# A two-layer trunk kernel on one core: float32 products in one matmul each instead of three float32r ones, and a longer ring of weight tiles

## The chip, the core and the metric

The kernel runs on one core of a Trainium2 chip. The core has a matrix engine (TensorE, PE in the profile; its weight loads are shown apart as PEld), a vector engine (VectorE, DVE), a scalar engine (ScalarE, ACT), a general engine (GpSimd, POOL) and SyncE (SP), whose queue issues nearly all of the transfers here. The metric is the device time of one execution in microseconds (us). Before the change it is 2586.55 us, the median of three runs from 2581.08 to 2590.38 us.

## What is computed

256 latent tokens `x` and 256 context tokens `ctx`, each 2048 wide, go through two layers. In both, the tokens are normalized and modulated by a condition vector, multiplied by a wide input matrix, mixed along the sequence, gated, multiplied by an output matrix and added to the stream. Only the latent tokens leave the second layer.

```
# layer 1 of the reference (called layer 0 in the kernel)
hx = modulate(x, norm, sh, sc) @ w_in            # 16 + 24 + 9 column blocks of 128
o_na  = neighbourhood_attention(...)              # 8 heads of 128
o_mla = mla_latent_attention(...)                 # 8 heads, from ranks of 512
x = x + gt * ((concat(o_na, o_mla) * silu(z)) @ w_out)
# layer 2 (layer 1 in the kernel)
h = modulate(x, norm, sh, sc) @ w_in              # keys, queries, values, gates z
q, k, v = silu(depthwise_conv(qkv)), q and k normalized per head
o = gated_delta_chunked(...) in both directions   # 32 heads, chunks of 64 tokens
x = x + gt * ((rmsnorm(o) * silu(z)) @ w_out)
out = rmsnorm(x)
```

Everything is float32. The weights come from memory once, in tiles of 128 rows by 1024 columns.

## The kernel before

Features lie on the 128 partitions and tokens along the free axis, so that one matmul multiplies a 128x128 block of weights by 128x512 activations (both sequences) or 128x256 (latent tokens alone) and adds the product to a PSUM bank. One such block is called a **k-step** below; 16 k-steps make a column block of 128 outputs, 32 in the last output matrix.

The chip's float32 matmul is not used for these products. A weight tile `raw` is rounded by ScalarE to a float32r tile `whi` (line 77) and VectorE makes the remainder `wlo` (line 78); the activations are held as `hh` and `hl` likewise, made in `modulate`. A k-step in `dense` is then three float32r matmuls: high by high (line 90), high by low (line 91), low by high (line 92). `product` (line 346) does the same in the attention, `pd` (line 713) has two such matmuls for the decays, and the state's update in `step` (line 1013) has three for each half of the partitions. Many smaller products are plain float32 already: the permutation `pp` of the rotary embedding (line 434), the sums `pg` (line 660), the modulations `pmod` (line 127), `pks` (line 982), `ptr` (lines 994 and 1027).

The stages in order: the modulations and the gate units `z` of layer 0, in seven groups of feature tiles (`sliced`, up to about 200 us); eight neighbourhood heads, the latent ranks and eight latent heads (`attend`), with the modulation weights of both layers as filler; the output matrix (`gh`, `gl`); modulation 2, which writes `hh` and `hl` anew; the keys and queries of layer 1 (`head`, `inverse`; from about 1130 us on); the scans with the value units as filler (`step`, from about 1800 us on); and the rest of the output matrix.

Outside the scans a scheduler orders each engine's instructions. In the scans (lines 1156 to 1244) PE, VectorE and ScalarE follow the order of the code: `step` yields four times, and between its parts the loop takes 3, 2 and 3 k-steps of a value unit (`cut`). `hi()` and `lo()` make the parts of the next weight tile there, `finish` normalizes and gates a head, stores the result to memory (`god`) and `gate` loads it again and splits it to `gh` and `gl` for the output products. SP's queue runs in order; a load into a tile of a ring waits there until the tile's last reader is done. The ring `raw` has four tiles, `whi` and `wlo` three each.

```
            PE.matmul(ps, wh[:, c], xh[:, k0 + k, sl], start=first and k == 0, stop=False)
            PE.matmul(ps, wh[:, c], xl[:, k0 + k, sl], start=False, stop=False)
            end = PE.matmul(ps, wl[:, c], xh[:, k0 + k, sl], start=False, stop=last and k == kt - 1)
```

Of the kernel before, what the change touches and what calls it, by code (L numbers as in the profile page):

```python
# [16 lines left out]
KT = 16  # L17
S = 256
# [8 lines left out]
def trunk_kernel(ctx: ExitStack, tc: tile.TileContext, g):  # L27
# [4 lines left out]
    wp = ctx.enter_context(tc.tile_pool(name="wp", bufs=2))  # L32
    big = ctx.enter_context(tc.tile_pool(name="big", bufs=1))
# [34 lines left out]
    # ---------------------------------------------------------------- helpers  # L68
    def load_raw(src, n=1024):
        raw = wp.tile([128, 1024], F32, name="raw", tag="raw", bufs=4)  # L70
        nc.sync.dma_start(raw[:, :n], src)
        return raw

    def split(raw, m=1024):
        hi = wp.tile([128, 1024], F32R, name="whi", tag="whi", bufs=3)
        lo = wp.tile([128, 1024], F32R, name="wlo", tag="wlo", bufs=3)
        A.copy(hi[:, :m], raw[:, :m])  # L77
        V.tensor_tensor(lo[:, :m], raw[:, :m], hi[:, :m].bitcast(F32), op=ALU.subtract)  # L78
        return hi, lo

    def load_split(src, n=2048):
        return [split(load_raw(src[:, c:min(n, c + 1024)], min(1024, n - c)), min(1024, n - c))
                for c in range(0, n, 1024)]

    def dense(ps, w, off, kt, xh, xl, k0=0, sl=slice(0, T), first=True, last=True):
        for k in range(kt):
            c = off + k * 128
            wh, wl = w[c // 1024]
            c = slice(c % 1024, c % 1024 + 128)
            PE.matmul(ps, wh[:, c], xh[:, k0 + k, sl], start=first and k == 0, stop=False)  # L90
            PE.matmul(ps, wh[:, c], xl[:, k0 + k, sl], start=False, stop=False)  # L91
            end = PE.matmul(ps, wl[:, c], xh[:, k0 + k, sl], start=False, stop=last and k == kt - 1)  # L92
        return end.ins

    def sliced(wsrc, units, k0, n, xh, xl, pst, first, last):
        # n contraction tiles of two units
        m = 128 * n
        raw = wp.tile([128, 1024], F32, name="raw", tag="raw", bufs=4)
        for e in range(2):
            nc.sync.dma_start(raw[:, m * e:m * e + m], wsrc[units[e]][:, 128 * k0:128 * k0 + m])  # L100
        w = split(raw, 2 * m)
        for e in range(2):
            dense(pst[e], [w], m * e, n, xh, xl, k0=k0, first=first, last=last)
# [1273 lines left out]
```

## Time and profile before

| what | value |
|---|---|
| median of the runs shown | 2586.55 us (2581.08 to 2590.38) |
| span of the profiled execution, first to last instruction | 2580.0 us |
| mean granted TensorE clock in it | 0.985 |
| PE busy from 0 to 70 us | 48.16 us |
| PE busy from 70 to 200 us | 130.00 us |
| PE busy from 1130 to 1800 us (keys and inverses) | 638.54 of 670 us, DVE 594.62, clock 0.96 |
| PE busy from 1800 to 2440 us (scans) | 635.45 of 640 us, DVE 462.61, clock 1.00 |
| PE busy from 2463 to 2570 us (last output products) | 105.10 of 107 us |

The profiled execution has no time of its own beside the span; 6.55 us lie between the span and the median of the timed runs. In the rows of the profile `A*B` is the part of the array that a matmul uses (rows by columns), `128x512 f32` its output, and `xN` a number of records. float32r tiles show as f32 too; the line tells them apart. The end of a matmul's record is modelled, so its duration includes the way through the array, and consecutive records overlap; the time that a matmul holds the engine is read from the distance between starts.

### The profile page before, as it was taken

How to read it: one execution, taken by the hardware profiler on the slowest of the kernel's cores; microseconds unless marked ns; L12 is line 12 of the kernel's file. 1: busy time of each engine (PE TensorE's matmuls, PEld its weight loads, DVE VectorE, ACT ScalarE, POOL GpSimd, SP SyncE). 2: the span in 40 equal slices, each digit the busy share in tenths (PEclk: the TensorE clock that was granted, in tenths of full speed). 3: DMA queues.
4: the chain of work that ended last, by engine and by line, in shares of the span. 5: the costliest groups of instructions: out<-in, count | busy, mean ns of one | idle time of the engine just before them, and what ended most of it. 6: DMA issues, size and time to landing. Idle time of an engine off the chain costs nothing.

```text
span 2580.0 us, 43446 instructions
## 1 busy us (share of the span) xinstructions
PE 2499.2 (97%) x16586; PEld 2039.0 (79%) x16586; DVE 1852.2 (72%) x3543; ACT 1146.6 (44%) x2484; POOL 267.4 (10%) x261
## 2 busy tenths in 40 slices
PE   6999999999999999989999999999999999999998
PEld 4657888888767788768888889897777777777898
DVE  4544788773455687758999999987677777777754
ACT  4223323232333422377656655643444445445353
POOL 0000000000000000133212222310000000003000
PEclk9999999999999999999999999999999999999999
DMA  8872655532343376644454544563333433335454
GB/s 258 289 247 90 201 172 167 175 114 96 117 153 100 120 230 221 212 139 157 142 156 152 160 138 150 159 213 100 88 99 115 119 99 106 113 91 174 153 188 140
DMA packets 201810, 394.30 MB, mean 153 GB/s; under 512 B 68225, under 2 KB 109697, under 8 KB 201473
## 3 DMA queue, kind: packets, MB, share of 16 engines
q1 hardware_dynamic: 200448, 389.98, 47.9%
q8 instruction: 131, 2.15, 0.4%
q10 hardware_dynamic: 1152, 1.54, 0.2%
q14 instruction: 79, 0.64, 0.1%
HBM read 356.28 MB, written 35.13 MB: 152 GB/s over the span
## 4 chain that ended last, share of the span: by engine, by line
PE 79%; DVE 9%; issue 6%; DMA 3%; ACT 2%; SPq 0%; POOL 0%; DVEq 0%; POOLq 0%; ACTq 0%
PE mm L90 19%; PE mm L91 18%; PE mm L92 18%; PE pks L982 3%; PE pmod L127 3%; DVE wlo L78 2%; PE sp L348 2%; PE ptr L994 2%; DVE X L770 1%; DVE outer L768 1%; PE po L348 1%; PE pu L798 1%; DVE acc L561 1%; PE ptr L1027 1%; PE psu L1013 1%
## 5 line engine op out<-in xcount | busy, mean ns | idle before, releaser
L90 PE MATMUL mm<-hh,whi 128*128 128x512 f32 (+1 forms) x2784 | 988.5, 355 | 3.7 <-ACT t L636 2.2
L92 PE MATMUL mm<-hh,wlo 128*128 128x512 f32 (+1 forms) x2784 | 962.2, 346 | 8.7 <-DVE wlo L78 7.5
L91 PE MATMUL mm<-hl,whi 128*128 128x512 f32 (+1 forms) x2784 | 963.2, 346 | 0.0
L77 ACT CAST whi<-raw 128x1024 fp32r<-128x1024 f32 (+2 forms) x346 | 338.3, 979 | 668.4 <-PE mm L91 515.6
L90 PEld LDWEIGHTS mm<-hh,whi 128*128 128x128 f32 x2784 | 535.7, 192 | 113.8 <-issue 32.6
L92 PEld LDWEIGHTS mm<-hh,wlo 128*128 128x128 f32 x2784 | 535.4, 192 | 73.1 <-DVE wlo L78 9.4
L91 PEld LDWEIGHTS mm<-hl,whi 128*128 128x128 f32 x2784 | 536.0, 193 | 62.2 <-issue 8.4
L78 DVE TENSOR_TENSOR wlo<-raw,whi 128x1024 fp32r<-128x1024 f32 (+2 forms) x346 | 402.7, 1166 | 212.9 <-ACT whi L77 206.1
L163 DVE SCALAR_TENSOR_TENSOR lacc<-mraw,cond,lacc 128x512 f32<-128x512 f32 x300 | 208.8, 749 | 0.0
L561 DVE SCALAR_TENSOR_TENSOR acc<-cin,taps,acc 128x508 f32<-128x508 f32 (+3 forms) x256 | 196.1, 767 | 6.7 <-ACT acc L552 4.3
L1004 DVE SCALAR_TENSOR_TENSOR vl<-ptr,egm,vh 128x128 fp32r<-128x128 f32 x224 | 64.6, 346 | 98.3 <-ACT rf L1001 39.4
L711 POOL TENSOR_TENSOR rhs<-ghl,incl 128x512 fp32r<-128x512 f32 (+1 forms) x96 | 108.4, 1139 | 133.4 <-PE pd L713 114.2
L127 PE MATMUL pmod<-mraw,cond 128*32 128x512 f32 (+2 forms) x640 | 94.3, 501 | 23.2 <-DMA mraw<-ab_wm 18.6
L768 DVE SCALAR_TENSOR_TENSOR outer<-L,bv,X 128x31 f32<-128x31 f32 (+15 forms) x248 | 112.4, 453 | 4.7
L1088 DVE TENSOR_TENSOR wlo<-raw,whi 128x1024 fp32r<-128x1024 f32 x84 | 102.6, 1222 | 14.4 <-ACT whi L1080 13.8
L194 POOL TENSOR_TENSOR rs<-ms,half 128x4 f32<-128x4 f32 (+1 forms) x5 | 4.7, 947 | 985.1 <-DVE ms L192 985.1
L770 DVE TENSOR_TENSOR X<-X,outer 128x31 f32<-128x31 f32 (+15 forms) x248 | 101.7, 410 | 4.6
L575 ACT ACTIVATE ac<-acc 128x128 f32<-128x128 f32 x160 | 37.4, 300 | 146.0 <-DVE acc L561 146.0
L90 PE MATMUL mm<-gh,whi 128*128 128x512 f32 x256 | 99.9, 392 | 1.7 <-DVE x1B L493 1.7
L91 PE MATMUL mm<-gl,whi 128*128 128x512 f32 x256 | 99.9, 390 | 0.2 <-DVE gl L481 0.2
L92 PE MATMUL mm<-gh,wlo 128*128 128x512 f32 x256 | 99.7, 390 | 0.0
L998 ACT ACTIVATE vh<-ptr,egm 128x128 fp32r<-128x128 f32 x224 | 71.0, 373 | 56.6 <-PE ptr L994 54.6
(289 smaller groups left out, 3629.2 us busy)
## 6 DMA issues: line engine op xcount, KB each, us to landing
raw<-dn_w SPq DMA_DIRECT2D x194, 512.0 KB, 4.0
mraw<-dn_wm SPq DMA_DIRECT2D x96, 512.0 KB, 4.7
mraw<-ab_wm SPq DMA_DIRECT2D x88, 512.0 KB, 5.4
raw<-ab_w SPq DMA_DIRECT2D x66, 512.0 KB, 3.8
raw<-dn_wo SPq DMA_DIRECT2D x64, 512.0 KB, 3.7
raw<-ab_wo SPq DMA_DIRECT2D x32, 512.0 KB, 4.6
raw<-ab_w SPq DMA_DIRECT2D x32, 256.0 KB, 3.6
spt<-sp SPq DMA_DIRECT2D x64, 128.0 KB, 2.8
```

The lines of the kernel that those rows point to most:

```text
L77: A.copy(hi[:, :m], raw[:, :m])
L78: V.tensor_tensor(lo[:, :m], raw[:, :m], hi[:, :m].bitcast(F32), op=ALU.subtract)
L90: PE.matmul(ps, wh[:, c], xh[:, k0 + k, sl], start=first and k == 0, stop=False)
L91: PE.matmul(ps, wh[:, c], xl[:, k0 + k, sl], start=False, stop=False)
L92: end = PE.matmul(ps, wl[:, c], xh[:, k0 + k, sl], start=False, stop=last and k == kt - 1)
L127: PE.matmul(pmod[32 * q:32 * q + 32, :m], cond[:, 4 * kg + q, :], raw[c // 1024][:, half + c % 1024:half + c % 1024 + m], start=kg == 0, s ...
L163: V.scalar_tensor_tensor(acc[:, s], raw[:, q], cond[:, k, s:s + 1], acc[:, s], op0=ALU.mult, op1=ALU.add)
L561: V.scalar_tensor_tensor(o3[:, :, i0:i1], p3[:, :, i0 + d:i1 + d], taps[:, ch, t:t + 1], o3[:, :, i0:i1], op0=ALU.mult, op1=ALU.add)
L711: P.tensor_tensor(rhs, ghl[i].bitcast(F32)[:, d, kh * 8:kh * 8 + 2 * n].unsqueeze(2).broadcast_to(sh), incl[:, c].unsqueeze(1).broadcast_t ...
L768: V.scalar_tensor_tensor(o, L[:, rows, k:k + 1].broadcast_to([128, n, m]), bv[:, k:k + 1], X[:, k:k + 1, cols].broadcast_to([128, n, m]), ...
L770: V.tensor_tensor(X[:, rows, cols], X[:, rows, cols], o, op=ALU.subtract)
L1088: V.tensor_tensor(w, raws[j], h.bitcast(F32), op=ALU.subtract)
```

## The change

Every product takes its float32 operands as they are. `dense` has one matmul for a k-step; `split`, `hi`, `lo`, `both`, `parts`, `product` and `split_keys` are gone, with all tiles that held low parts. The ring of weight tiles, now the only one, has ten tiles (`RAWS`). `modulate` writes its result with two instructions for each feature tile and sequence, in layer 1 into the tile `x1` that it reads. The output matrix of layer 0 reads the gated outputs `go2` where they are. In layer 1 `finish` writes the gated outputs of all 32 heads into one tile `gob`, which the output products read; the stores to `god`, the loads back and `gate` are gone.

```diff
-    def split(raw, m=1024):
-        hi = wp.tile([128, 1024], F32R, name="whi", tag="whi", bufs=3)
-        lo = wp.tile([128, 1024], F32R, name="wlo", tag="wlo", bufs=3)
-        A.copy(hi[:, :m], raw[:, :m])
-        V.tensor_tensor(lo[:, :m], raw[:, :m], hi[:, :m].bitcast(F32), op=ALU.subtract)
-        return hi, lo
...
-            PE.matmul(ps, wh[:, c], xh[:, k0 + k, sl], start=first and k == 0, stop=False)
-            PE.matmul(ps, wh[:, c], xl[:, k0 + k, sl], start=False, stop=False)
-            end = PE.matmul(ps, wl[:, c], xh[:, k0 + k, sl], start=False, stop=last and k == kt - 1)
+            end = PE.matmul(ps, w[c // 1024][:, c % 1024:c % 1024 + 128], x(k0 + k, sl),
+                            start=first and k == 0, stop=last and k == kt - 1)
...
-        raw = wp.tile([128, 1024], F32, name="raw", tag="raw", bufs=4)
+        raw = wp.tile([128, 1024], F32, name="raw", tag="raw", bufs=RAWS)
...
-                A.activation(hh[:, k, sl], h[:, sl], AF.Identity, bias=shift)
-                if k % 3 == 2:
-                    V.scalar_tensor_tensor(hl[:, k, sl], h[:, sl], shift, hh[:, k, sl].bitcast(F32),
-                                           op0=ALU.add, op1=ALU.subtract)
-                else:
-                    A.activation(h[:, sl], h[:, sl], AF.Identity, bias=shift)
-            if k % 3 != 2:
-                P.tensor_tensor(hl[:, k], h, hh[:, k].bitcast(F32), op=ALU.subtract)
+                V.scalar_tensor_tensor(h[:, k, sl], src(k, s), Am[l][:, k, s:s + 1], rb[:, sl], op0=ALU.mult, op1=ALU.mult)
+                A.activation(h[:, k, sl], h[:, k, sl], AF.Identity, bias=mods[l][:, k, s:s + 1])
...
-                    product(sp[:, :N], lambda i: qT[:, i, q0:q0 + 128], lambda i: kT[:, i, c0:T], True, rope is None)
+                    PE.matmul(sp[:, :N], qT[:, q0:q0 + 128], kT[:, c0:T], start=True, stop=rope is None)
...
-                for i in range(2):
-                    rhs = tp.tile([128, 8, 64], F32R, name="rhs", tag="rhs")[:, :2 * n]
...
-                    PE.matmul(pd, seg[:, c], rhs.rearrange("p u i -> p (u i)"), start=i == 0, stop=i == 1)
+                rhs = tp.tile([128, 8, 64], F32, name="rhs", tag="rhs")[:, :2 * n]
...
+                PE.matmul(pd, seg[:, c], rhs.rearrange("p u i -> p (u i)"), start=True, stop=True)
...
-                for i, (x, y) in enumerate(((0, 0), (0, 1), (1, 0))):
-                    for h in range(2):
-                        r = slice(64 * h, 64 * h + 64)
-                        PE.matmul(psu[h].rearrange("p h v -> p (h v)"), ksp[r, s, x, t],
...
+                for h in range(2):
+                    r = slice(64 * h, 64 * h + 64)
+                    PE.matmul(psu[h].rearrange("p h v -> p (h v)"), o.kt[r, t], vs[r].rearrange("p h v -> p (h v)"),
+                              start=True, stop=True, tile_position=(64 * h, 0))
...
-            o.go = gos[o.kh % 2]
+            o.go = gob[:, 2 * o.kh:2 * o.kh + 2]
...
-            if o.kh < 14:
-                nc.sync.dma_start(god[:, 2 * o.kh:2 * o.kh + 2], o.go)
...
+        def ahead_of(j):
+            while len(raws) < min(len(W), j + RAWS):
+                raws.append(load(W[len(raws)]))
```

The first place is PE's row of work inside the scans, where a value unit's k-steps (`mm`) stand between the parts of a chunk's step: here before the update of the context's state (`pks` and `ptr` from the values `vh`, `vl` and the keys `ksp`). Before:

```order
L90 MATMUL mm<-hh,whi 128x512
L91 MATMUL mm<-hl,whi 128x512
L92 MATMUL mm<-hh,wlo 128x512
L1013 MATMUL pks<-vh,ksp 128x256
L1013 MATMUL ptr<-vh,ksp 128x256
L1013 MATMUL pks<-vl,ksp 128x256
L1013 MATMUL ptr<-vl,ksp 128x256
```

The third pair of the update (high values by low keys) follows, and reads like the first. PE's row at the same kind of place now (`x` is the modulated tile, `kt` the keys as loaded, `ptr<-rh,rc` the end of the latent tokens' chunk):

```order
L1127 MATMUL pvv<-ident,ac_12608 128x128 x4
L81 MATMUL mm<-x_4275,raw 128x512 x2
L953 MATMUL pks<-vh,kt_10529 128x256
L953 MATMUL ptr<-vh,kt_10529 128x256
L81 MATMUL mm<-x_4275,raw 128x512 x3
L966 MATMUL ptr<-rh,rc 128x128 x2
```

A k-step's three rows have become one, and the six of a state's update two; the numbers of k-steps between two parts of the chain (2, then 3) are the same.

The second place is SP's queue at the start, where the loads of the first weight slices (`raw`, with the number of their buffer) stand among those of the modulation weights (`mraw`) of the second feature tile. Before, two slices being one tile of the ring:

```order
L122 DMA mraw_239<-ab_wm 128x4x128 x2
L122 DMA mraw_250<-ab_wm 128x4x128 x2
L100 DMA raw_355<-ab_w 128x128
L100 DMA raw_372<-ab_w 128x128 x2
L100 DMA raw_389<-ab_w 128x128 x2
L122 DMA mraw_281<-ab_wm 128x4x128 x2
L122 DMA mraw_309<-ab_wm 128x4x128 x2
```

And now:

```order
L114 DMA mraw_236<-ab_wm 128x4x128 x2
L93 DMA raw_313<-ab_w 128x128
L93 DMA raw_322<-ab_w 128x128 x2
L93 DMA raw_331<-ab_w 128x128 x2
L93 DMA raw_340<-ab_w 128x128 x2
L93 DMA raw_347<-ab_w 128x128 x2
L93 DMA raw_371<-ab_w 128x128 x2
L93 DMA raw_404<-ab_w 128x128 x2
L93 DMA raw_434<-ab_w 128x128 x2
L93 DMA raw_451<-ab_w 128x128 x2
L114 DMA mraw_259<-ab_wm 128x4x128 x2
L114 DMA mraw_279<-ab_wm 128x4x128 x2
```

Before, the last four loads of these modulation weights stand behind seven tiles of the ring of four; now they stand behind thirteen tiles of the ring of ten. `raw_404`, `raw_434` and `raw_451` are the eleventh to thirteenth.

More of the change, by code (lines that the diff above doesn't have):

```diff
@@ L81, in load_split, with loads, dense @@
[L81 to L85, printed above, removed]
+    def loads(src, n=2048):
+        return [load(src[:, c:min(n, c + 1024)], min(1024, n - c)) for c in range(0, n, 1024)]
+    def dense(ps, w, off, kt, x, k0=0, sl=slice(0, T), first=True, last=True):
         for k in range(kt):
             c = off + k * 128
[L88 to L92, printed above, removed]
+            end = PE.matmul(ps, w[c // 1024][:, c % 1024:c % 1024 + 128], x(k0 + k, sl),
+                            start=first and k == 0, stop=last and k == kt - 1)
@@ L102, in sliced @@
         for e in range(2):
-            dense(pst[e], [w], m * e, n, xh, xl, k0=k0, first=first, last=last)
+            dense(pst[e], [raw], m * e, n, x, k0=k0, first=first, last=last)
     mod_loads = []
@@ L1202, in trunk_kernel @@
             take(C, 1)
-            hi()
             take(dn, cut[0])
```

240 lines of the change are left out of this document (83 added, 157 removed).

## The prediction

> **What bounds the kernel now.** I read the page's busy line first, then the rows of PE's matmuls by line and shape, then starts on the timeline, and PE's waits last.
>
> ```profile
> span 2580.0 us, 43446 instructions
> PE 2499.2 (97%) x16586; PEld 2039.0 (79%) x16586; DVE 1852.2 (72%) x3543; ACT 1146.6 (44%) x2484; POOL 267.4 (10%) x261
> ```
>
> PE is idle for 2580.0 - 2499.2 = 80.8 us; no other engine comes near that. Since matmul records overlap, 97% alone doesn't say that the array is full. The distance between starts does:
>
> ```profile
> 1856.34 0.39 PE L92 MATMUL mm<-hh,wlo 128*128 128x512 f32 x1
> ...
> 1857.71 0.39 PE L92 MATMUL mm<-hh,wlo 128*128 128x512 f32 x1
> 1501.49 0.28 PE L90 MATMUL mm<-hh,whi 128*128 128x256 f32 x1
> ...
> 1502.34 0.28 PE L91 MATMUL mm<-hl,whi 128*128 128x256 f32 x1
> ```
>
> From the first row to the second are six float32r matmuls of 512 columns, 1.37 us, so 0.228 us each (I use 0.227); from the third to the fourth seven of 256 columns, 0.85 us, so 0.12 us each. A k-step of three takes **0.681 us** with 512 columns and **0.36 us** with 256. How many there are:
>
> ```profile
> L90 PE MATMUL mm<-hh,whi 128*128 128x512 f32 x1504 | 613.0, 408 | 0.6 <-DVE zs L292 0.5
> L90 PE MATMUL mm<-hh,whi 128*128 128x256 f32 x1280 | 375.5, 293 | 3.1 <-ACT t L636 2.2 <-ACT whi L1080 0.9
> L90 PE MATMUL mm<-gh,whi 128*128 128x512 f32 x256 | 99.9, 392 | 1.7 <-DVE x1B L493 1.7
> L90 PE MATMUL mm<-ch,whi 128*128 128x512 f32 x112 | 46.6, 417 | 0.0
> L90 PE MATMUL pz<-hh,whi 128*128 128x512 f32 x64 | 25.2, 415 | 1.3 <-ACT hh L222 1.3
> ```
>
> 1504 + 256 + 112 + 64 = **1936** k-steps of 512 columns and **1280** of 256. They take 1936 x 0.681 + 1280 x 0.36 = 1318 + 461 = 1779 us of PE, 69% of the span, issued back to back. So the kernel is bound by the time for which matmuls hold the array, and the change is decided by one price: a plain float32 matmul against three float32r ones.
>
> **That price.** The kernel already has plain float32 matmuls:
>
> ```profile
> L434 PE MATMUL pp<-rope,ropet 128*128 128x256 f32 x10 | 3.2, 400 | 0.0
> 657.87 0.39 PE L90 MATMUL mm<-hh,whi 128*128 128x512 f32 x1
> 658.10 0.59 PE L434 MATMUL pp<-rope,ropet 128*128 128x256 f32 x2
> 658.34 0.58 PE L91 MATMUL mm<-hl,whi 128*128 128x512 f32 x1
> 658.76 0.39 PE L92 MATMUL mm<-hh,wlo 128*128 128x512 f32 x1
> 1131.81 1.95 PE L660 MATMUL pg<-gst,cumh 128*128 128x128 f32 x16
> 1133.51 0.47 PE L90 MATMUL mm<-hh,whi 128*128 128x512 f32 x1
> 1133.82 0.39 PE L91 MATMUL mm<-hl,whi 128*128 128x512 f32 x1
> ```
>
> Line 434 is executed five times (once for the key, four for the queries) and has ten records: a float32 product is **two records**. The pair at 658.10 has 256 columns. L92 starts at 658.76, and L91 ahead of it needs its 0.227, so the pair held the array until 658.53: 0.43 us, 0.215 a record, nearly twice the 0.12 of float32r with the same columns. (L91's early start at 658.34 is only its record's.) Likewise the sixteen records with 128 columns at 1131.81 held it until 1133.82 - 0.227 = 1133.59: 1.78 / 16 = 0.111 each. From 128 to 256 columns a record grows by 0.104; two more steps of 0.104 to 0.109 give 0.423 to 0.433 for 512. The only float32 rows with 512 columns are those of `pmod`, where four narrow matmuls run side by side:
>
> ```profile
> 1106.67 1.06 PE L127 MATMUL pmod<-mraw,cond 128*32 128x512 f32 x8
> 1107.66 0.50 PE L91 MATMUL mm<-hl,whi 128*128 128x512 f32 x1
> ...
> 2324.08 0.60 PE L982 MATMUL pks<-St,kq 128*64 128x256 f32 x4
> 2324.61 0.50 PE L90 MATMUL mm<-hh,whi 128*128 128x512 f32 x1
> ```
>
> Eight records are two rounds, 0.99 us with the change back to the full array. That change is seen at 2324.08: two rounds of 0.215 and the change make 0.53, so the change is 0.10, and a round of `pmod` 0.445. Bounds for a record of 512 columns: 0.423 to 0.445. I take 0.433, the upper end of the line through full-array rows, to which the new matmuls are nearest. A k-step is then **0.866 us** with 512 columns (+0.185) and 0.435 with 256 (+0.075): slower than the three.
>
> The Perfetto Trace Analysis page of the Trainium skill, in the footnote to Engine Utilization, halves the array's output rate for FP32_LOW_HIGH; by it a k-step of 512 columns would be two times 0.227 = 0.454, and the change a gain. The pair at 658.10, 0.43 for 256 columns where half rate would be 0.24, disagrees.
>
> **The change part by part**, against the span of 2580.0:
>
> 1. k-steps with 512 columns: 1936 x 0.185 = **+358** (bounds 1936 x 0.165 = 319 and 1936 x 0.209 = 405).
> 2. k-steps with 256: 1280 x 0.075 = **+96** (90 to 102).
> 3. Attention, decays and state updates:
>
> ```profile
> L348 PE MATMUL sp<-kT,qT 128*128 128x512 f32 x96 | 28.4, 408 | 0.0
> L348 PE MATMUL sp<-kr,qr 64*128 64x512 f32 x48 | 15.4, 427 | 0.0
> L348 PE MATMUL po<-PT,vt 128*128 128x256 f32 x288 | 46.4, 289 | 0.7 <-ACT PT L340 0.7
> L713 PE MATMUL pd<-rhs,seg 128*128 128x512 f32 x64 | 23.6, 404 | 0.0
> L1013 PE MATMUL ptr<-vh,ksp 64*128 64x256 f32 x224 | 58.8, 315 | 0.4 <-DVE vl L1004 0.3 <-ACT whi L1080 0.2
> ```
>
> A third of the first two rows, 48 products of 512 columns, costs 48 x 0.185 = 9; the same number of 256 (the context's queries) and 96 of `po` cost 144 x 0.075 = 11. The decays had two matmuls: 32 products go from 0.46 to 0.866, +13, and the 16 half as wide +3. The 224 rows of `vh` are two for an update: 112 updates, each from three side-by-side pairs of 0.12 to two of 0.215, +0.07, +8. Together **+44** (40 to 50).
>
> 4. What goes from the other engines: the splitting of weights.
>
> ```profile
> L77 ACT CAST whi<-raw 128x1024 fp32r<-128x1024 f32 (+2 forms) x346 | 338.3, 979 | 668.4 <-PE mm L91 515.6
> L78 DVE TENSOR_TENSOR wlo<-raw,whi 128x1024 fp32r<-128x1024 f32 (+2 forms) x346 | 402.7, 1166 | 212.9 <-ACT whi L77 206.1
> PE pmod L127 <- DMA mraw<-ab_wm: 18.6, 8, 16.0
> PE ptk L679 <- ACT ac L572: 15.2, 7, 3.7
> PE mm L92 <- DVE wlo L78: 7.5, 8, 2.4
> PE qss L689 <- ACT km L686: 5.5, 2, 3.6
> PE pmod L127 <- DMA mraw<-dn_wm: 4.5, 5, 1.4
> ```
>
> 741 us of ScalarE and VectorE work go, but they lay beside PE. PE's waits show what they were worth: 7.5 us for `wlo`, and about 6 for other low or rounded parts, which lie below these rows. Those 13 go. The waits for `ptk`, `qss` and `dn_wm` (25 us) shrink, as engines ahead of PE have less to do while its work between them is 27% longer; I take half. Together **-26**, from 0 to -57: of 80.8 us of idle time, 16.0 are the first wait at the start and about 8 follow the last matmul. The gated outputs kept on chip and modulation 2 in place are inside this term too.
>
> 5. Ten tiles in flight. SP's queue is in order, and at the start thirteen tiles now stand ahead of the second feature tile's last four modulation loads (seven before).
>
> ```profile
> 26.76 2.51 SPq L100 DMA_DIRECT2D raw<-ab_w  x5
> 29.38 3.25 SPq L122 DMA_DIRECT2D mraw<-ab_wm  x4
> 29.86 1.97 PE L90 MATMUL pz<-hh,whi 128*128 128x512 f32 x4 [1.26 <-ACT hh L222]
> ```
>
> The eleventh to thirteenth must wait until PE has read the first three, six k-steps: 29.86 + 6 x 0.866 = 35.1. So these loads go out some 6 us after 29.38, and the `pmod` that needs them, with everything behind it in PE's order, stands behind eight k-steps and four other matmul rounds, about 39 us. With landing it is late by 0 to 6 us; **+3**. Later in the kernel weights arrive early in both versions, and I cost the ring at nothing; what it costs if that fails is a rival below.
>
> Sum: 358 + 96 + 44 - 26 + 3 = +475, a span of 3055. The timed median lies 6.55 us above the profiled span before; the same again gives **3062 us**. Lower ends of all terms (319 + 90 + 40 - 57 + 0) give 2978, upper ends (405 + 102 + 50 + 0 + 6) 3150.
>
> **The rivals.**
>
> *Long records*: a float32 record of 512 columns costs what `pmod` shows, 0.445. For it: those are the only rows with 512. Against it: four streams run there at once. +47 on the first term and some 7 on the others: 3116.
>
> *The ring turns into a wait*: a load for a ring tile now waits until PE has read the tile ten places before, and in the scans each head's keys and inverses are queued behind such loads. A small load of that kind takes 2.6 us to land:
>
> ```profile
> rg<-spk SPq DMA_DIRECT2D x16, 256.0 KB, 2.6
> ```
>
> If every one of 16 heads came late by that, and nothing of the 26 were relieved, 3062 + 26 + 42 + 3 = 3133. Against it: a head's loads are issued four steps, over 30 us, ahead (640 us from 1800 us on hold some 70 steps).
>
> *More relief*: all 57 us of idle time inside go (31 more), and the clock (the last number but two, 0.96) returns to 1.00 in the stage of keys and inverses, another 27 of its 670 us: 3004.
>
> ```profile
> 1130.00:1800.00 670.00, 638.54 (x6017) 575.44 (x6016) 594.62 (x977) 400.47 (x785) 162.78 (x170) 0.96 0.49 150
> ```
>
> For it: PE would have no gaps. Against it: the many 32x32 matmuls there stay.
>
> *Not slower, half rate*: the pair of records takes as long as two float32r matmuls. Then 1936 x 0.227 + 1280 x 0.12 + about 28 = 621 us go instead, 1940 us in the end; VectorE's 1852 less its splitting doesn't stand in the way. It decides from the point where a record with 512 columns takes under 0.34 us. This is what the page's footnote would make of it. The pair of `pp` speaks against it.
>
> **How the numbers follow.** Forecast 0.64, long records 0.13, the ring as a wait 0.11, more relief 0.08, half rate 0.04. The last alone is faster; with a quarter of it I allow that new waits eat the gain, so faster by over 0.3% (about what a measurement of this kernel can tell from no change) 0.03, within 0.3% 0.01, slower 0.96. The range takes the ends of the sum, 2978 to 3150, with a little room, and holds the three slower rivals.
>
> **What would show it.** Right: line 81 with 2 x 1936 records of 512 columns at starts 0.43 apart and 2 x 1280 of 256 at 0.215 to 0.22; PE's idle time near 55 us; the scans' step longer by eight times 0.185. Wrong: starts 0.445 or more apart (long records), or 0.23 (half rate); PE idle behind DMA rows of `raw` or of a head's loads (the ring); PE's first 70 us with more idle time than 22 us (the start).

## The result: 16% slower, and where the time came from

The changed kernel takes **3004.16 us** (median; 3002.19 to 3005.51) against 2584.95 us of the kernel before, measured on the same chip (2581.08 to 2590.38). The ratio is 1.1621 with a 95% interval of [1.1604, 1.1637]. The direction and the mechanism of the forecast hold; the forecast of 3062 us is 58 us too high.

The page of the changed kernel, first its busy line (share of the span, number of instructions of each engine), further down the chain of work that ended last:

```profile
span 3000.3 us, 33888 instructions
PE 2938.1 (98%) x12954; PEld 1669.7 (56%) x12954; DVE 1207.0 (40%) x2711; ACT 691.5 (23%) x1904; POOL 123.9 (4%) x150
...
PE 90%; issue 5%; DMA 2%; DVE 2%; ACT 1%; SPq 0%; POOL 0%; DVEq 0%; POOLq 0%; ACTq 0%
```

DVE went from 1852 to 1207 us and ACT from 1147 to 692, yet the span grew by 420 us. PE has fewer instructions, 12954 for 16586, and is busy 439 us longer. Its idle time is 3000.3 - 2938.1 = 62.2 us, 18.6 less than before. So PE still sets the end, and what it does takes longer.

The groups of PE's matmuls by line and shape, those of the k-steps (line 81 is `dense` now):

```profile
L81 PE MATMUL mm<-x,raw 128*128 128x512 f32 x1568 | 722.1, 602 | 0.0
L81 PE MATMUL mm<-x,raw 128*128 128x256 f32 x1536 | 356.7, 387 | 2.7 <-ACT t L595 2.7
L81 PE MATMUL mm<-hh,raw 128*128 128x512 f32 x1440 | 639.0, 595 | 0.0
L81 PE MATMUL mm<-gob,raw 128*128 128x256 f32 x1024 | 229.2, 381 | 0.0
L81 PE MATMUL mm<-go,raw 128*128 128x512 f32 x512 | 223.0, 594 | 0.0
L81 PE MATMUL mm<-ch,raw 128*128 128x512 f32 x224 | 103.6, 602 | 0.0
L81 PE MATMUL pz<-hh,raw 128*128 128x512 f32 x128 | 63.1, 635 | 1.3 <-ACT hh L212 1.3
```

The shapes 128x512 add up to 3872 records, twice 1936, and 128x256 to 2560, twice 1280: every plain float32 product is two records. How long one holds the array is read from starts on PE's timeline (start, duration, records):

```profile
1254.58 23.34 PE L81 MATMUL mm<-go,raw 128*128 128x512 f32 x54
1277.76 1.84 PE L162 MATMUL pml<-ones,lacc 128*128 128x1 f32 x16
...
2804.81 4.48 PE L81 MATMUL mm<-gob,raw 128*128 128x256 f32 x20
2809.13 0.61 PE L966 MATMUL ptr<-rh,rc 128*128 128x128 f32 x4
```

54 records in 23.18 us are **0.429 us** each, 20 in 4.32 us **0.216**. A k-step takes 0.858 and 0.432 us, against 0.681 and 0.36 of the three float32r matmuls.

With these prices the change can be summed stage by stage. The marks are first or last records of named matmuls, the same in both traces; the price is the number of k-steps between the marks in each trace times their length, plus the other products that became float32.

| from mark to mark | before, us | after, us | price of the products | what is left |
|---|---|---|---|---|
| start to first k-step | 29.9 | 29.1 | 0 | -0.8 |
| to the first `sp` (gate units) | 270.6 | 323.8 | +53.8 | -0.6 |
| to the last `po` (attention) | 605.0 | 714.5 | +125.5 | -16.0 |
| to `pg` (output matrix, modulation 2) | 226.3 | 294.5 | +53.4 | +14.8 |
| to the first value `pvv` (keys, inverses) | 623.4 | 700.8 | +113.9 | -36.5 |
| to the last `pvv` (scans) | 599.4 | 677.4 | +95.9 | -17.9 |
| to the end | 225.3 | 260.4 | +35.3 | -0.2 |
| sum | 2579.9 | 3000.3 | +477.8 | -57.2 |

The last stage, almost nothing but k-steps, grows by its price to 0.2 us. Three stages gave something back, above all the keys, and one has a new wait. The price counts k-steps and products alone, so other work that changes its stage shows in the last column. One group did: of the modulation records `pmod`, 128 stand in the attention before (26.8 us, summed from each start to the next) and 96 now (20.3 us); the other 32 have gone to the next stage. So some 6.5 us of the attention's -16.0, and of the +14.8 behind it, are work that moved. PE's waits (engine, line, what it waited for: us in total, times, longest) name that wait:

```profile
PE pmod L119 <- DMA mraw<-ab_wm: 21.7, 11, 15.4
PE pmod L119 <- DMA mraw<-dn_wm: 11.7, 4, 6.2
PE ptk L635 <- ACT ac L532: 10.6, 2, 5.3
PE mm L81 <- ACT t L595: 2.7, 1, 2.7
```

The waits for `wlo` are gone, and `ptk` waits 10.6 us for 15.2. `dn_wm`, the weights of modulation 2, went up from 4.5 to 11.7. The timeline shows it in one place, the last chunks ahead of layer 1:

```profile
1322.06 1.91 PE L119 MATMUL pmod<-mraw,cond 128*32 128x512 f32 x12
1330.17 4.64 PE L119 MATMUL pmod<-mraw,cond 128*32 128x512 f32 x12 [6.19 <-DMA mraw<-dn_wm]
1335.68 1.05 PE L119 MATMUL pmod<-mraw,cond 128*32 128x512 f32 x4 [0.88 <-DMA mraw<-dn_wm]
1338.69 1.92 PE L119 MATMUL pmod<-mraw,cond 128*32 128x512 f32 x4 [1.95 <-DMA mraw<-dn_wm]
```

Brackets hold the idle time ahead of a row and what ended it. In the windows of this stretch (length, then busy time and instructions of PE, PEld, DVE, ACT and POOL, granted clock, DMA share, GB/s) the clock falls too:

```profile
1320.00:1362.00 42.00, 29.48 (x97) 13.79 (x97) 8.12 (x20) 11.25 (x24) 4.13 (x6) 0.80 0.38 122
```

### The profile page after: what moved, and what is told of

The parts are those of the page before. It is cut to its first block, busy times and chain, and to the rows that moved or that the text cites. A ratio compares the mean times of both kernels' runs of the same rounds, so it can differ in the third digit from the quotient of the medians.

```text
span 3000.3 us, 33888 instructions
## 1 busy us (share of the span) xinstructions
PE 2938.1 (98%) x12954; PEld 1669.7 (56%) x12954; DVE 1207.0 (40%) x2711; ACT 691.5 (23%) x1904; POOL 123.9 (4%) x150
## 4 chain that ended last, share of the span: by engine, by line
PE 90%; issue 5%; DMA 2%; DVE 2%; ACT 1%; SPq 0%; POOL 0%; DVEq 0%; POOLq 0%; ACTq 0%
PE mm L81 67%; PE pks L927 3%; PE pmod L119 3%; PE pz L81 2%; PE ptr L939 2%; PE sp L339 1%; PE po L360 1%; DMA mraw<-ab_wm 1%; PE pu L753 1%; PE px L741 1%; PE pks L953 1%; PE psu L953 1%; PE ptr L966 1%; PE sp L342 1%; PE pd L668 1%
## 5 line engine op out<-in xcount | busy, mean ns | idle before, releaser
L81 PE MATMUL mm<-x,raw 128*128 128x512 f32 (+1 forms) x3104 | 1076.4, 496 | 2.7 <-ACT t L595 2.7
L81 PEld LDWEIGHTS mm<-x,raw 128*128 128x128 f32 x3104 | 576.0, 192 | 374.6 <-issue 327.3
L81 PE MATMUL mm<-hh,raw 128*128 128x512 f32 x1440 | 639.0, 595 | 0.0
L81 PEld LDWEIGHTS mm<-hh,raw 128*128 128x128 f32 x1440 | 267.6, 190 | 324.2 <-issue 311.0
L81 PE MATMUL mm<-gob,raw 128*128 128x256 f32 x1024 | 229.2, 381 | 0.0
L81 PE MATMUL mm<-go,raw 128*128 128x512 f32 x512 | 223.0, 594 | 0.0
L81 PEld LDWEIGHTS mm<-gob,raw 128*128 128x128 f32 x1024 | 191.7, 190 | 32.5 <-issue 7.9
L81 PEld LDWEIGHTS mm<-go,raw 128*128 128x128 f32 x512 | 96.2, 190 | 121.5 <-issue 120.7
L119 PE MATMUL pmod<-mraw,cond 128*32 128x512 f32 (+2 forms) x640 | 93.9, 509 | 33.6 <-DMA mraw<-ab_wm 21.7
L961 DVE SCALAR_TENSOR_TENSOR St<-St,eglb,psu 128x128 f32<-128x128 f32 x96 | 29.1, 345 | 206.4 <-PE ptr L953 206.4
L943 ACT ACTIVATE vh<-ptr,egm 128x128 f32<-128x128 f32 x224 | 71.2, 374 | 152.5 <-PE ptr L939 150.6
L81 PE MATMUL mm<-ch,raw 128*128 128x512 f32 x224 | 103.6, 602 | 0.0
```

Source lines behind the costliest of these rows:

```text
L81: end = PE.matmul(ps, w[c // 1024][:, c % 1024:c % 1024 + 128], x(k0 + k, sl), start=first and k == 0, stop=last and k == kt - 1)
L119: PE.matmul(pmod[32 * q:32 * q + 32, :m], cond[:, 4 * kg + q, :], raw[c // 1024][:, half + c % 1024:half + c % 1024 + m], start=kg == 0, s ...
L943: A.activation(vs[:, e], ptr[:, e], AF.Copy, scale=egm[:, a, u0 + e:u0 + e + 1])
```

## The experiments

Two theories stood for the 57 us that the stages gave back: **lighter engines** (VectorE and ScalarE no longer make low parts) and **longer work of TensorE** (the same chains beside it now fit). For the two losses, the start and modulation 2, the rings of tiles were suspected.

### 1. Four weight tiles instead of ten

```diff
-    RAWS = 10
+    RAWS = 4
```

> The changed kernel with four tiles in the ring of weights instead of ten. Theory (array time alone decides, the ring gave nothing): no k-step gets longer, and PE's waits for modulation weights, 21.7 + 11.7 = 33.4 us in the changed kernel against 18.6 + 4.5 = 23.1 before, fall back by 5 to 10 us: 2994 to 3000 us. Rival (ten tiles are what keeps the weights early): waits for raw tiles appear, 3010 us or more.

Measured: 2993.66 us (2990.14 to 2993.96), ratio 1.158 [1.1547, 1.1613]; 10.5 us less than the changed kernel. 8.0 of them lie between the first k-step and the first `sp` (315.8 for 323.8 us); the attention is the same, 714.5 us. So the ten tiles cost time at the start, and nothing elsewhere needed them. But the waits, from which the expectation had the gain, fell by 2 us only (21.1 + 9.9 for 21.7 + 11.7). The windows show a stretch from 70 to 200 us that has gaps in the changed kernel, where before had none, and smaller ones with four tiles. First the rows of the changed kernel:

```profile
0.00:70.00 70.00, 50.28 (x279) 21.06 (x280) 24.62 (x56) 18.17 (x26) 1.22 (x5) 1.00 0.81 247
70.00:200.00 130.00, 125.32 (x447) 44.79 (x446) 38.25 (x84) 8.43 (x20) 0.00 (x0) 0.99 0.69 236
```

and with four tiles:

```profile
70.00:200.00 130.00, 128.14 (x485) 47.06 (x484) 41.28 (x89) 8.42 (x20) 0.00 (x0) 0.99 0.75 255
```

With four tiles the first 70 us have more idle time in return (PE busy 48.27 us), so that up to 200 us PE is idle for 23.6 us, against 24.4: gaps explain about one of the 8 us. Most of the rest lies in how the modulations are cut up. A piece of four `pmod` records among k-steps holds PE from 1292.34 to 1293.32 in the changed kernel:

```profile
1292.34 1.05 PE L119 MATMUL pmod<-mraw,cond 128*32 128x512 f32 x4
1293.32 3.70 PE L81 MATMUL mm<-x,raw 128*128 128x512 f32 x8
```

That is 0.98 us, as long as the piece of eight at 1106.67 in the prediction (0.99). Between the first k-step and the first `sp`, PE takes 128 such records in 25 pieces with ten tiles (24.7 us from start to next start) and in 19 with four (18.8 us).

### 2. The splits made again, read by nobody

On top of experiment 1, ScalarE rounds every weight tile and VectorE makes its remainder, as before the change:

```diff
+    def hi_lo(raw, m=1024):
...
+        A.copy(hi[:, :m], raw[:, :m])
+        V.tensor_tensor(lo[:, :m], raw[:, :m], hi[:, :m].bitcast(F32), op=ALU.subtract)
...
```

> The ring of four, and for every weight tile ScalarE's rounding and VectorE's remainder are made as before, into tiles that nothing reads; some 430 instructions on each of the two engines. Theory (those engines only have to be free, and are): within 8 us of the ring of four alone. Rival (the 37 us by which PE's waits shrank more than forecast came from the relieved engines, in the chains that PE waits for): 20 to 40 us above the ring of four.

Measured: 3005.80 us (2999.36 to 3019.11), ratio 1.1637 [1.1593, 1.1681], 12 us above experiment 1 in the same comparison, between the two expectations. The keys are 9.3 us longer (707.0 for 697.7). The attention is 6.9 longer and modulation 2 5.4 shorter, but that is mostly work that moved: 120 modulation records stand in the attention here, 96 in experiment 1. The load of the splits brings back a part of what was given back, and not most of it.

### 3. The gated outputs through memory again

Each pair of gated outputs is stored to `god` and loaded into `gob`, on top of the changed kernel.

```diff
...
+            nc.sync.dma_start(god[:, 2 * o.kh:2 * o.kh + 2], o.go)
+            nc.sync.dma_start(gob[:, 2 * o.kh:2 * o.kh + 2], god[:, 2 * o.kh:2 * o.kh + 2])
```

> The changed kernel, but each head's gated output goes to memory and back into the tile on chip (32 stores and 32 loads of 256 KB on SP's queue). Theory (keeping it on chip was worth nothing beside PE): 3002 to 3008 us. Rival (the store and load were on the path): 3015 us or more, with PE idle in the last 200 us before the output products.

Measured: 3004.72 us, ratio 1.1622 [1.1582, 1.1662], the changed kernel's own 1.1621. Keeping them on chip is worth nothing that can be measured here.

### 4. The kernel before with float32 value units

```diff
+                if j < NV:
+                    PE.matmul(p, raws[j][:, 128 * k:128 * k + 128], xh[:, k0 + k, sl].bitcast(F32),
+                              start=first and k == 0, stop=last and k == 7)
+                else:
...
```

> The kernel before, with one part of the change alone: the 480 k-steps of the value units in the scans (512 columns) are one float32 matmul of the unsplit weights by the high part of the activations; the low parts are left out of these products. All splitting work stays. Theory (a k-step costs 2 x 0.429 instead of 3 x 0.227): 480 x 0.177 = +85 us, 2668 to 2672 us, the step of the scans longer by 8 x 0.177 = 1.4 us. Rival (a float32 record is as short as in the changed kernel only when VectorE and ScalarE don't split): +95 us or more. Rival (the chain between PE's parts hides some of it): +70 us or less.

Measured: 2653.74 us (2652.03 to 2656.14), ratio 1.0268 [1.0239, 1.0298], +72.7 us: the expected sum was 12 too high. Some 6 of them are a price that was wrong for before. In the scans its float32r matmuls are not 0.227 apart, as the timeline of before shows:

```profile
1900.94 0.40 PE L92 MATMUL mm<-hh,wlo 128*128 128x512 f32 x1
...
1902.33 0.40 PE L92 MATMUL mm<-hh,wlo 128*128 128x512 f32 x1
```

Six matmuls lie between these rows, 1.39 us, 0.232 each; over the scans the median is 0.231, a k-step 0.693. With 0.858 - 0.693 = 0.165 the 480 k-steps cost 79 us, not 85. Before also has two pairs of scan steps that are longer than the others (22.42 and 24.49 us among a median of 19.71 from one `ptr<-rh,rc` to the next, 7.5 us in all); with float32 values one such remains (27.06 among 22.17, 4.9 us). That leaves 4 us or so unexplained.

### 5. Eight tiles for the modulation weights

With four weight tiles as in experiment 1, and eight tiles in place of three in the other ring:

```diff
-    def adaln(l, ps, pm, tp, order, bufs=3, after=None):
+    def adaln(l, ps, pm, tp, order, bufs=8, after=None):
...
-                    raw = tp.tile([128, 2, 512], F32, name="mraw", tag="mraw", bufs=3)
+                    raw = tp.tile([128, 2, 512], F32, name="mraw", tag="mraw", bufs=8)
```

> The changed kernel with four weight tiles in flight, and eight modulation tiles mraw in flight in place of three wherever three were. Theory: the waits of pmod (line 119) for dn_wm, and the half clock that follows them, come from the loads of modulation 2 standing behind a ring of three tiles that a denser stretch of products now releases late; with eight tiles they land ahead, the stretch from the last po to pg falls from 297 to about 280 us, and the kernel comes to 2976 to 2984 us against 2993.7 with three. Rival: the loads are held by the place in SP's order at which they are issued, or by bandwidth, and not by tiles; then the stretch stays and the time is within 4 us of 2993.7.

Measured: 2965.13 us (2961.87 to 2966.42), ratio 1.1489 [1.147, 1.1508]; 28.5 us under experiment 1. The stage from the last `po` to `pg` falls from 297.0 to 267.8 us, which is all of it. PE has no row of waits for `dn_wm` any more, and the last modulations run in one piece, as its timeline shows (32 records without a gap, where the changed kernel had 12, 12, 4 and 4 with waits):

```profile
1294.02 3.64 PE L119 MATMUL pmod<-mraw,cond 128*32 128x512 f32 x32
```

So the loads were held by the ring of three tiles. The gain is larger than expected, and larger than the waits. Here are two windows with three tiles (experiment 1), where the stage ends at 1356.5 us, and then with eight, where it ends at 1322.3 and the second window is already in the keys:

```profile
1055.00:1330.00 275.00, 265.85 (x730) 117.42 (x728) 123.26 (x230) 25.41 (x51) 1.01 (x1) 0.98 0.57 189
1330.00:1365.00 35.00, 29.75 (x97) 18.12 (x98) 8.57 (x22) 15.32 (x39) 4.13 (x6) 0.80 0.25 82
```

```profile
1055.00:1330.00 275.00, 273.68 (x781) 129.72 (x780) 110.84 (x218) 40.65 (x90) 5.59 (x7) 0.99 0.49 162
1330.00:1365.00 35.00, 35.00 (x184) 22.98 (x186) 12.13 (x23) 21.92 (x55) 9.28 (x10) 1.00 0.37 118
```

Idle time goes from 9.15 + 5.25 = 14.4 to 1.3 us, and the clock from 0.98 and 0.80 to 0.99 and 1.00. That is worth at most another 275 x 0.01 + 35 x 0.20 = 10 us, and less as far as PE was idle while the clock was low. At least 6 of the 29 are left. The 32 modulation records that had moved into this stage are back in the attention, which is no longer for it (712.6 for 714.5 us): its 128 records, in longer pieces, take 20.5 us from start to next start, where 96 took 20.3. This is the fastest of the float32 versions tried, and 15% slower than before.

### 6. Products that wait for their split

As experiment 2, but the products outside the scans read the tile that VectorE makes:

```diff
-        V.tensor_tensor(lo[:, :m], raw[:, :m], hi[:, :m].bitcast(F32), op=ALU.subtract)
+        V.tensor_tensor(lo[:, :m], raw[:, :m], hi[:, :m], op=ALU.max)
+        return lo
...
```

> The kernel with four weight tiles whose splits are still made (3005.8 us), but with the products outside the scans reading the tile that VectorE makes at the end of the split (values unchanged: the larger of the weight and its copy). Engine load as there; new is only that a product waits for its split as it did before the change. Theory: the waits for the split are what the changed kernel was relieved of in the keys and in the attention; the time rises by 10 to 30 us, to 3015 to 3035, in those two stages. Rival: the relief comes from the lighter engines and the clock, not from the wait itself; then within 8 us of 3005.8.

Measured: 2998.62 us (2998.31 to 3000.21), ratio 1.1618 [1.1601, 1.1635], 7 us below experiment 2, not above. At TensorE's float32 pace no cost of waiting for a split shows; the theory that the wait was what the change removed finds no support. The keys take 698.8 us, 1 us more than in experiment 1, though the splits are made here too, so experiment 2's 9 us there are not firm either.

### 7. Two of the three matmuls

The kernel before, without line 91:

```diff
-            PE.matmul(ps, wh[:, c], xl[:, k0 + k, sl], start=False, stop=False)
```

> The kernel before with two of its three matmuls in each dense k-step: the weight's high part by the activations' low part is left out, which drops the activations' low parts there. Theory: TensorE bounds every dense stage, so the time falls by 1936 x 0.2285 + 1280 x 0.12 = 596 us, to about 1985 us. Rival: VectorE, which works 595 of 670 us in the keys, becomes the bound there, TensorE waits for wlo, and the time is 2050 to 2080 us with the excess in the stage from pg to the first value.

Measured: 2355.03 us, ratio 0.9124 [0.91, 0.9148]: 226 us less (two executions, 2351.86 and 2358.19), where both theories expected over 500. PE's longest waits, and the windows from keys to values and over the scans:

```profile
PE px L785 <- DVE U L775: 59.6, 7, 23.2
PE pml L169 <- DVE lacc L162: 39.7, 4, 20.4
PE kk L726 <- ACT sp L698: 27.5, 6, 6.0
PE pd L712 <- POOL rhs L710: 23.7, 45, 1.7
```

```profile
1010.00:1608.00 598.00, 491.82 (x4345) 422.64 (x4343) 524.57 (x857) 347.03 (x708) 143.84 (x158) 0.81 0.51 157
```

```profile
1608.00:2177.00 569.00, 518.68 (x3525) 386.41 (x3525) 459.42 (x1149) 287.80 (x868) 63.34 (x58) 0.93 0.40 117
```

Every stage stops short: keys and inverses save 24.6 of 146 us, the attention 77 of 141, the scans 31 of 120 (each the matmuls that the stage has fewer, by 0.2285 or 0.12 us). PE is idle and its clock falls, to 0.81 in the keys. The page splits the 370 us that are missing: PE's idle time is 2356.3 - 2048.7 = 307.6 us, 227 more than before, and its busy time shrank by 450 us, not 596; the other 145 go with the clock, 0.901 in the mean for 0.985. So in the kernel before TensorE is the bound with other engines close behind it, closest in the keys, where VectorE works 525 of 598 us in this version.

### 8 and 9. One engine lighter, the other's work longer

Two edits of the kernel before separate the two theories. Experiment 8 takes VectorE's remainders away and leaves TensorE as it is:

```diff
-        lo = wp.tile([128, 1024], F32R, name="wlo", tag="wlo", bufs=3)
...
-        V.tensor_tensor(lo[:, :m], raw[:, :m], hi[:, :m].bitcast(F32), op=ALU.subtract)
-        return hi, lo
+        return hi, hi
...
```

> The kernel before without the remainders of the weights: the third matmul of a k-step reads the high part a second time, so TensorE's work is the same, and the weights' low parts are left out. VectorE has 505 us less to do (402.7 + 102.6) and no product waits for wlo. Theory A (the relief in the changed kernel comes from the lighter VectorE): 20 to 45 us less than before, 2536 to 2561 us, most of it from pg to the first value (623 us). Theory B (it comes from TensorE's longer work, beside which the other engines' chains fit): the waits for wlo alone go, 8 to 15 us, 2566 to 2573.

Experiment 9 adds the fourth product and leaves the other engines as they are:

```diff
+            PE.matmul(ps, wl[:, c], xl[:, k0 + k, sl], start=False, stop=False)
             end = PE.matmul(ps, wl[:, c], xh[:, k0 + k, sl], start=False, stop=last and k == kt - 1)
```

> The kernel before with a fourth float32r matmul in each k-step, low by low, which adds 1936 x 0.2285 + 1280 x 0.12 = 596 us of TensorE's work (k-steps of 0.91 and 0.48 us) and nothing on the other engines: splits, waits and rings stay. Theory B (longer work of TensorE alone takes up the waits and the half clock, as the changed kernel's 0.858 did): 40 to 55 us less than the sum, 3122 to 3137 us, with keys and attention each 20 to 40 us under their part of it. Theory A (relief needs lighter engines): the stages grow by their full parts, 3165 to 3180.

Measured: 8 takes 2549.60 us, ratio 0.9863 [0.9836, 0.989], 35 us less than before; the keys are 29 us shorter (594.3 for 623.4). 9 takes 3124.74 us, ratio 1.2093 [1.2066, 1.212]: +540 of 596, 56 given back. By the matmuls that stand between the marks in each trace, 30 of them are in the keys (+117.4 of 147), 12 in the scans and 11 between the first k-step and the first `sp`, where the modulations of 512 columns now stand in 18 pieces for 27. The attention gives nothing back (+139.7 of 137), against the expectation. The windows of the keys in 8, in 9 and in the changed kernel:

```profile
1140.00:1734.00 594.00, 586.42 (x5590) 530.13 (x5589) 424.56 (x819) 384.96 (x746) 150.63 (x165) 0.99 0.52 162
```

```profile
1396.00:2137.00 741.00, 728.54 (x6601) 667.08 (x6600) 578.19 (x947) 383.64 (x740) 171.99 (x166) 0.99 0.43 130
```

```profile
1362.00:2062.00 700.00, 688.24 (x4571) 488.53 (x4571) 411.40 (x814) 248.72 (x601) 95.91 (x116) 0.99 0.45 137
```

Before, VectorE worked about nine tenths of this stage and PE had a clock of 0.96 and over 30 us of idle time. In all three windows PE idles 8 to 12 us at 0.99, with VectorE at 424.56 of 594, 578.19 of 741 and 411.40 of 700. Either edit alone, a lighter VectorE or a longer TensorE, gives back some 30 us in the keys. Both theories are right there, and they don't add: the changed kernel does both and gives back 36.5. It fits all three that what counts is how near VectorE's work is to the stage's length, and also experiment 2, which lost little with VectorE at 553 of 706 us. One thing is not separated: experiment 8 takes away the wait for `wlo` together with VectorE's load, and experiment 6 tests the wait alone only at the float32 pace.

### 10 and 11. Remainders on GpSimd

If VectorE's load costs the kernel before 35 us, part of it might be had with the same values:

```diff
-        V.tensor_tensor(lo[:, :m], raw[:, :m], hi[:, :m].bitcast(F32), op=ALU.subtract)
+        nsplit.append(0)
+        (P if len(nsplit) % 3 == 0 else V).tensor_tensor(lo[:, :m], raw[:, :m], hi[:, :m].bitcast(F32), op=ALU.subtract)
```

> The kernel before, with the remainder of every third weight tile outside the scans made by GpSimd in place of VectorE; the same values. Theory (VectorE's load between pg and the first value, 560.8 of 620 us, is what holds TensorE there by about 30 us): some 42 of 127 remainders of 1.17 us leave VectorE there, 49 us, a third of what the kernel without remainders took off, and a third of its 35 us comes back: 8 to 15 us less than before, 2570 to 2577. Rival: GpSimd takes over 2 us for one (its rhs of half the size takes 1.05), and products wait for those; then no gain or a loss, 2580 to 2600.

> The same with every second remainder on GpSimd. Theory: 12 to 20 us less than before, 2565 to 2573. Rival: GpSimd, at over 2 us each for some 64 remainders beside its 159 us there, is late with rhs and the pd products behind it; slower than with every third, 2580 to 2620.

Measured: 2638.07 us with a third, ratio 1.022 [1.0206, 1.0234], and 2656.60 us with half, 1.0292 [1.0278, 1.0306]. Both are slower, beyond the ranges of the rivals too; with a third moved the keys take 681.0 us for 623.4. The group of GpSimd's remainders, and then VectorE's groups within the keys (1140 to 1780 us), with a third moved:

```profile
L81 POOL TENSOR_TENSOR wlo<-raw,whi 128x1024 fp32r<-128x1024 f32 (+2 forms) x115 | 279.6, 2431 | 1078.3 <-ACT whi L79 991.8 <-DMA raw<-ab_w 21.6 <-PE sp L351 17.4
```

```profile
L771 DVE SCALAR_TENSOR_TENSOR outer<-L,bv,X 128x31 f32<-128x31 f32 (+15 forms) x233 | 127.9, 549 | 5.6
L773 DVE TENSOR_TENSOR X<-X,outer 128x31 f32<-128x31 f32 (+15 forms) x233 | 110.3, 473 | 5.4
L564 DVE SCALAR_TENSOR_TENSOR acc<-cin,taps,acc 128x510 f32<-128x510 f32 (+3 forms) x120 | 101.2, 843 | 6.0 <-ACT acc L555 5.4
```

The same groups of the kernel before, within its keys (1140 to 1750 us):

```profile
L768 DVE SCALAR_TENSOR_TENSOR outer<-L,bv,X 128x31 f32<-128x31 f32 (+15 forms) x236 | 107.8, 457 | 4.4
L770 DVE TENSOR_TENSOR X<-X,outer 128x31 f32<-128x31 f32 (+15 forms) x235 | 97.5, 415 | 4.2
L561 DVE SCALAR_TENSOR_TENSOR acc<-cin,taps,acc 128x510 f32<-128x510 f32 (+3 forms) x124 | 87.3, 704 | 0.6 <-ACT acc L552 0.3
```

GpSimd takes 2.43 us for a remainder, VectorE 1.17, and these groups of VectorE became longer by 14 to 20%: the steps of the inverses (`outer`, `X`) and the taps. Most of what VectorE was spared is eaten by that (57 us of remainders less in these windows, 47 us more in the three groups). Single instructions show how. Here are two taps of the same size on VectorE, and GpSimd's remainder that began just ahead of the first:

```profile
1319.49 2.87 DVE L564 SCALAR_TENSOR_TENSOR acc<-cin,taps,acc 128x510 f32<-128x510 f32 x1
1322.83 0.74 DVE L564 SCALAR_TENSOR_TENSOR acc<-cin,taps,acc 128x510 f32<-128x510 f32 x1
1319.43 2.39 POOL L81 TENSOR_TENSOR wlo<-raw,whi 128x1024 fp32r<-128x1024 f32 x1
```

The tap beside the remainder ends 0.54 us after it and takes 2.87 us; the other takes 0.74. This explains that nothing was won. The 57 us lost in the keys lie in PE's idle time (62 us for 30) and its clock (0.93 for 0.97); the longest wait there is that of `ptk` for ScalarE's `ac`, 31.8 us for 15.2. `ac` is made from what the taps give, which fits, but no run tests that chain by itself.

### 12. Only the attention's own products in float32

In the kernel before:

```diff
-            for i, (x, y) in enumerate(((0, 0), (0, 1), (1, 0))):
-                PE.matmul(ps, a(x), b(y), start=first and i == 0, stop=last and i == 2)
+            PE.matmul(ps, a(0).bitcast(F32), b(0).bitcast(F32), start=first, stop=last)
```

> The kernel before with only the attention's own products as one float32 matmul of the high parts each (their low parts are made and left unread). In the changed kernel the attention grew by 109.5 us where its k-steps alone account for 619.7 x 0.177 = 109.7, as if its own products (48 of 512 columns, 144 of 256) had cost nothing. Theory: they cost the array what k-steps do, 48 x 0.177 + 144 x 0.072 = 19 us, and the changed kernel paid it but was relieved of as much there by lighter engines; then the attention grows from 605 to about 624 us and the kernel comes to about 2600. Rival: in these short chains a product's price is hidden in the time around it (other products, changes of the tile), and the attention stays within 6 us of 605.

Measured: 2594.16 us, ratio 1.0042 [1.0025, 1.0059]. The attention takes 624.0 us for 605.0. That it is exactly the 19 of the theory is in part luck: four k-steps (2.7 us) have left the attention, and its modulation records take 4.0 us longer (30.7 for 26.8); without both it would be 18. But the products' price is real, and the rival of a hidden price falls. In the whole only 12 us show: the output matrix and modulation 2 came out 7 us longer (233.7; half of it is k-steps that came over), and the keys, which the edit doesn't touch either, 14 shorter (609.1), with PE idle for 22 us there in place of 30. So the stages of before vary by that much with what stands ahead of them, and a gain of under 15 us in the keys can't be put down to one cause.

## Why the prediction was right in direction and 58 us too high

1. **k-steps with 512 columns, forecast +358.** The mechanism and the count hold (2 x 1936 records). A record took 0.429 us, inside the bounds of 0.423 to 0.445 and below the chosen 0.433, which was the upper end of the line through full-array rows. With 0.858 - 0.681 the term is 1936 x 0.177 = **+343**.
2. **k-steps with 256, +96.** A record took 0.216: 1280 x 0.072 = **+92**.
3. **Attention, decays, state updates, +44.** With the same prices 19 + 16 + 8 = **+43**; experiment 12 bears out the 19 to a few us.
4. **Waits relieved, -26, bounds 0 to -57.** This is the step that failed. The prediction read what PE could win from the waits that it shows, row by row, and took half of some. The stages gave back some 65 us where they gained (72 in the table, less the modulations that moved), more than the lower bound. In the keys the wait rows held: the prediction's part for them, 7.5 us and half of 15.2 + 5.5, is 18 us, and PE's idle time fell by 18, from 30.1 to 11.8 us. But the stage gave back 36.5. What the prediction left out is the lower clock (0.97 in this stage, now 0.99: up to 10 us) and time inside stretches of matmuls that no wait row names (the rest). It treated the clock as a separate event, in the rival *more relief*. Experiments 8 and 9 show about 30 us for all this in the keys, reached by either cause. Against it stands modulation 2, +14.8 us in the table and some 8 without the work that moved there. Its wait for `dn_wm`, which the prediction had shrink, grew from 4.5 to 11.7 us, and experiment 5 shows that the ring of three tiles caused it. Net, with the 9 us or so of the ring counted under the next point, -66 stands for the -26.
5. **Ten tiles at the start, +3, bounds 0 to 6.** The direction holds, the size was 8 to 10 us (experiment 1). The place and the mechanism were wrong: the first 70 us have 70 - 50.28 = 19.7 us of idle time, under the 22 that were set as the mark, and up to 200 us the ten tiles leave PE idle for 1 us more than four do. Most of the cost is six more pieces of modulation at 0.98 us each, which the prediction didn't have in its sum.
6. **From the span to the median, +6.55.** It was 3004.16 - 3000.3 = 3.9.

In sum: 20 us of the miss are prices 1% too high, 34 are terms 4 and 5 (-57 for -23), 3 the median. The measured time lies on the number of the rival *more relief*, 3004, but not by its mechanism: it wanted all idle time inside to go, and 62.2 of 80.8 us are still there. *Long records* and *half rate* are excluded by the starts, and *the ring as a wait* by the windows of the scans, where PE is busy in all of the 678 us:

```profile
2062.00:2740.00 678.00, 678.00 (x3116) 363.62 (x3115) 286.41 (x801) 214.21 (x762) 15.89 (x16) 1.00 0.30 86
```

Three things stay open: some 8 of the 36.5 us in the keys, which no row names; some 7 of the attention's 16 (6.5 are modulations that moved, 1.9 the waits for `ch` and `PT` that are gone); and some 4 of the scans' 18 (6 are the price of before's k-steps there, 7.5 its long steps).

The FP8 and Floating Point Precision page of the Trainium skill, TensorE Precision Notes, says that true float32 makes four passes through the array, high and low by high and low. The starts come near that: 0.858 us against 0.908, four times the 0.227 of float32r. Experiment 9 is those four products spelled out, and it takes 3124.74 us.

## What to carry to other kernels

Price a change of operand type by the starts of a like instruction in the same trace, to the nanosecond where a thousand of them follow: here 1% of a record was worth 20 us. Where a second engine works nine tenths of a stage, don't read the whole possible gain from the wait rows (in the keys they held half of it): ask how long the stage would be if only one of the two engines worked, as experiments 8 and 9 do. When a stage gets denser, look at every ring that feeds it, the unchanged ones too: three modulation tiles cost 29 us here, and ten weight tiles cost 8 to 10 where four were enough. Before a stage's time is compared between two kernels, count its records: work that moved over a mark looks like time won on one side and lost on the other.

## What the runs showed of the hardware that was not expected

Plain float32 matmuls keep their distance of 0.429 us with 512 columns in every stage, scans included (the median of each stage), while float32r ones of before go from a median of 0.227 outside the scans to 0.231 within them.

A group of four side-by-side modulation records between k-steps holds PE for 0.98 us, as long as one of eight (0.99): six pieces more for the same 128 records cost 6 us in experiment 1's comparison.

A wait cost more than its length: at modulation 2, with three tiles, 14 us of idle time came with a lower clock (0.80 in the last 35 us) that is worth up to another 10. In all, the changed kernel with its longer work had a granted clock of 0.991 for the 0.985 of before.

GpSimd's subtraction beside VectorE made VectorE's instructions longer, 457 to 549 ns and 704 to 843. The SBUF — State Buffer page of the Trainium skill, in the section on its two separate sides, has VectorE with two inputs in SBUF and GpSimd take turns at a shared pair of ports, one blocked for the whole of the other's instruction. The trace agrees: the tap at 1319.49 beside GpSimd's remainder took 2.87 us, 2.13 more than the like one at 1322.83, and the remainder itself took 2.39.
